# A two-layer trunk in float32: the down projection in pairs of column blocks with seven-product pairs, and the feed-forward stage in three parts

## The chip, the cores and the metric

The kernel runs on one core of one Trainium2 chip. A core has TensorE (matrix products), VectorE (elementwise work on two operands), ScalarE (casts, copies, activation functions), GpSimd, and SyncE, whose queue (SP) issues nearly all DMA transfers here. The metric is the time of one execution on the device in microseconds (us); lower is better.

## The reference

A trunk of two layers over 256 tokens of width 2048. Each layer is a normalised mixer with a residual add, and then a normalised SwiGLU feed-forward stage with a residual add. Layer 0 mixes with sliding-window attention and an mLSTM, layer 1 with a forgetting attention. Only the feed-forward stage is touched here:

```python
FFN_HIDDEN = -(-(8 * D_MODEL) // (3 * 256)) * 256      # 5632

def swiglu(xn, w_gate, w_up, w_down):
    return (jax.nn.silu(xn @ w_gate) * (xn @ w_up)) @ w_down
...
        h = h + mix.astype(h.dtype)
        h = h + swiglu(rms_norm(h, norm_ffn[layer]), w_gate[layer], w_up[layer], w_down[layer])
    return rms_norm(h, norm_final)
```

All weights and activations are float32: `w_gate` and `w_up` are 2048 x 5632 per layer, `w_down` is 5632 x 2048.

## The kernel before

**A product in float32.** Each float32 operand is split into a rounded part and the rest (`hi` and `lo` for weights, `xh`/`xl` or `mh`/`ml` for activations), and a product is made of three matmuls: high by high, high by low, low by high (`three`, line 344). The split of a weight chunk of two k blocks by 512 columns (`split_chunk`, line 138) is one ScalarE cast (L141) and one VectorE subtraction (L142), both 128x1024. The 256 tokens are two tiles of 128, `t` = 0 and 1. So one chunk of 2 x 128 rows by 512 columns of a weight takes 2 k blocks x 2 token tiles x 3 = 12 matmuls of 128x512.

**Tiles.** Raw weights are loaded by SP into the pool `wr` with four tiles of 512 KB (L87), the split halves lie in `wp` with six `hi` and six `lo` tiles. PSUM has eight banks, four in the pool `pa` and four in `pm`.

**Gate and up.** The hidden width of 5632 is 11 blocks of 512 columns (`g`). `gate_up` makes one block of both products at once, over 8 pairs of k blocks in the order given by `ORDER`. Five pairs are plain: a chunk of `w_gate` and a chunk of `w_up`, 24 matmuls. Three pairs are mixed (pairs 2, 3 and 6): the 2x2 block product (two token tiles by two k blocks, two k blocks by the two matrices) is made by the Strassen-Winograd scheme with seven block products of three matmuls, 21 matmuls. For that VectorE forms four differences of raw weights in the tile `t4` (L378 to L381), splits of these follow (`ht`, `lt`, L240 and L241), and the sums of activations `sh`, `sl` were made earlier in `sums_of`. The seven products go to the four `plain` accumulators and four banks `mixed`. After the last pair, L405 to L409 combine the four banks (L406 is the first of VectorE's) and L413 adds the plain ones; the result goes through SiLU, a product with the up half, and eight transposes, and is split into `mh`, `ml` (or `eh`, `el` for k blocks from 16 on). With `par` the roles of the pools `pa` and `pm` change from block to block: the plain accumulators of a block take the banks that the mixed products of the block before had.

**Down.** `HALVES = (0, 6, 11)` cuts the 11 hidden blocks into two parts. After the gate/up blocks of a part, its share of the down projection follows: for each of four column blocks of 512 `gemm` runs over the part's 24 or 20 k blocks with plain chunks into two accumulators, and `add_out` (L246) adds to `h` (in the last part of layer 1 `finish`, L824 and on, with the gain `gf` loaded by GpSimd's queue, L447).

**Order.** The source gives instructions in program order, and a scheduler of the framework orders them on each engine's queue when the program is built, by priority, dependencies and free tiles. At run time every queue runs strictly in that built order. So an instruction that waits holds all behind it on its engine, and a load that waits for a free tile on SP holds all later loads.

Of the kernel before, what the change touches and what calls it, by code (L numbers as in the profile page):

```python
# [10 lines left out]
ALU = mybir.AluOpType  # L11
# [23 lines left out]
MIXED = [p for w, p in ORDER if w]  # L35
HALVES = (0, 6, 11)
# [3 lines left out]
def trunk(  # L40
# [128 lines left out]
    def x_of(k):  # L169
        return xh[:, k, :], xl[:, k, :]  # L170
# [28 lines left out]
    def sums_of(extra, pair, src):  # L199
        sh, sl, pool = extra  # L200
        full = pool.tile([P, 2, NT, P], F32, tag="tmp", name="full")
        for i in range(2):
            g = src[1][i]
            nc.scalar.mul(full[:, i, :, :].rearrange("p t q -> p (t q)"), src[0][i], g)
# [5 lines left out]
        j = MIXED.index(pair)  # L210
        split_plain(sh[:, j, :, :], sl[:, j, :, :], s)

    def split_scaled(idx, n, extra=None):
        for half in range(2):
            pt = pm.tile([P, 2, NT, P], F32, tag="pm", name="pt")
            for i in range(2):
                k = 4 * n + 2 * half + i
                for t in range(NT):
                    nc.tensor.transpose(pt[:, i, t, :], h[:, t, k * P : (k + 1) * P], ident)
# [8 lines left out]
            if extra is not None and 2 * n + half in MIXED:  # L228
                k = 4 * n + 2 * half
                sums_of(  # L230
                    extra,
                    2 * n + half,
                    (
                        [pt[:, i, :, :].rearrange("p t q -> p (t q)") for i in range(2)],
                        [gT[:, idx * KT + k + i : idx * KT + k + i + 1] for i in range(2)],
                    ),
                )
# [114 lines left out]
    def gate_up(fp, sh, sl, layer, g, par):  # L352
        c0 = g * NB
        plain = [[bank(par, "acc") for _ in range(NT)] for _ in range(2)]
        mixed = None
        count = [s_[0] for s_ in ORDER]
        for pos, (w, pair) in enumerate(ORDER):
            k0 = 2 * pair
            if not w:
                for m, wt in enumerate((w_gate[layer], w_up[layer])):  # L360
                    hi, lo = load_chunk(wt, k0, c0, NB)
                    for i in range(CK):
                        ah, al = x_of(k0 + i)
                        for t in range(NT):
                            ts = slice(t * P, (t + 1) * P)
                            three(
                                plain[m][t], ah[:, ts], al[:, ts], hi[:, i, :], lo[:, i, :],
                                pos == 0 and i == 0, pos == len(ORDER) - 1 and i == CK - 1,
                            )
                continue  # L370
            first, last = 1 not in count[:pos], 1 not in count[pos + 1 :]
            if first:
                mixed = [bank(1 - par, "prod") for _ in range(4)]
# [4 lines left out]
            nc.vector.tensor_tensor(out=t4[:, 0, :], in0=ru[:, 0, :], in1=rg[:, 0, :], op=ALU.subtract)  # L378
            nc.vector.tensor_tensor(out=t4[:, 1, :], in0=ru[:, 1, :], in1=ru[:, 0, :], op=ALU.subtract)  # L379
            nc.vector.tensor_tensor(out=t4[:, 2, :], in0=ru[:, 1, :], in1=t4[:, 0, :], op=ALU.subtract)  # L380
            nc.vector.tensor_tensor(out=t4[:, 3, :], in0=rg[:, 1, :], in1=t4[:, 2, :], op=ALU.subtract)  # L381
            hu = wp.tile([P, CK, NB], F32R, tag="hi", name="hi")
            lu = wp.tile([P, CK, NB], F32R, tag="lo", name="lo")
            split_plain(hu[:, 1, :], lu[:, 1, :], ru[:, 1, :])
# [7 lines left out]
            j = MIXED.index(pair)  # L392
            xa, la = x_of(k0)
            xb, lb = x_of(k0 + 1)
            t0, t1 = slice(0, P), slice(P, 2 * P)
            three(mixed[0], xa[:, t0], la[:, t0], hg[:, 0, :], lg[:, 0, :], first, last)
            three(plain[0][0], xb[:, t0], lb[:, t0], hg[:, 1, :], lg[:, 1, :], False, False)
            three(plain[1][0], sh[:, j, 3, :], sl[:, j, 3, :], hu[:, 1, :], lu[:, 1, :], False, False)
            three(mixed[1], sh[:, j, 0, :], sl[:, j, 0, :], ht[0], lt[0], first, last)
            three(mixed[2], sh[:, j, 2, :], sl[:, j, 2, :], ht[1], lt[1], first, last)  # L400
            three(mixed[3], sh[:, j, 1, :], sl[:, j, 1, :], ht[2], lt[2], first, last)
# [3 lines left out]
        nc.scalar.copy(c[:, 0, :], mixed[0])  # L405
        nc.vector.tensor_tensor(out=u2, in0=mixed[3], in1=c[:, 0, :], op=ALU.add)  # L406
        nc.vector.tensor_tensor(out=c[:, 1, :], in0=mixed[2], in1=u2, op=ALU.add)
        nc.vector.tensor_tensor(out=c[:, 2, :], in0=mixed[1], in1=u2, op=ALU.add)
        nc.vector.tensor_tensor(out=c[:, 3, :], in0=mixed[1], in1=c[:, 1, :], op=ALU.add)  # L409
        for m in range(2):  # L410
            for t in range(NT):
                o = c[:, 2 * m + t, :]
                nc.vector.tensor_tensor(out=o, in0=plain[m][t], in1=o, op=ALU.add)  # L413
        return c

    def ffn(layer, fp, sh, sl, eh, el, key, idx_next=None, key_next=None, finish=None):
        def a_of(k):
            return m_of(k) if k < KT else (eh[:, k - KT, :], el[:, k - KT, :])

        r = rstd(key)  # L420
        for part in range(2):
            g0, g1 = HALVES[part : part + 2]
            nk = 4 * (g1 - g0)
            for g in range(g0, g1):
                par = (g - g0 + part) % 2
                c = gate_up(fp, sh, sl, layer, g, par)
# [6 lines left out]
                for half in range(2):  # L433
# [5 lines left out]
                    k = 4 * (g - g0) + 2 * half  # L439
                    if k < KT:  # L440
                        split_plain(mh[:, k : k + 2, :], ml[:, k : k + 2, :], pt)
                    else:
                        split_plain(eh[:, k - KT : k - KT + 2, :], el[:, k - KT : k - KT + 2, :], pt)
            gf = None
            if part == 1 and finish is not None:
                gf = fp.tile([P, D], F32, tag="t4", name="gf", bufs=1)
                nc.gpsimd.dma_start(gf, norm_final.partition_broadcast(P))  # L447
            wd = w_down[layer][4 * g0 * P : 4 * g1 * P, :]
            for n in range(4):
                acc = new_acc()  # L450
                end = part == 1 and idx_next is None and n == 3
                gemm(acc, a_of, wd, n * NB, NB, 0, nk, nk, skew=3 if end else 1)
                if part == 0:
# [7 lines left out]

    def close_layer(layer, w_out, idx, key, **rest):
        with tc.tile_pool(name=f"fp{layer}", bufs=2) as fp:
            deep = max(4 * (b - a) for a, b in zip(HALVES, HALVES[1:])) - KT
            eh = fp.tile([P, deep, S], F32R, name="eh", bufs=1)
            el = fp.tile([P, deep, S], F32R, name="el", bufs=1)
            sh = fp.tile([P, len(MIXED), 4, P], F32R, name="sh", bufs=1)
            sl = fp.tile([P, len(MIXED), 4, P], F32R, name="sl", bufs=1)
            out_proj(w_out, idx, key, (sh, sl, fp))
            ffn(layer, fp, sh, sl, eh, el, key, **rest)  # L470
# [419 lines left out]
```

## Time and profile before

| | |
|---|---|
| median of 3 runs | 2177.47 us (2176.23 to 2179.84) |
| the profiled execution, its own time | 2177.11 us |
| its span | 2175.4 us |
| mean granted TensorE clock | 0.998 |
| raw loads of `w_gate`, `w_up`, `w_down` | 176 each, 512 KB each |
| median time to landing of these | 3.6, 4.5, 3.7 us |
| bytes moved, mean rate | 408.34 MB, 188 GB/s |

The span runs from the first to the last instruction of the profiled execution; its own time is a little longer, for what lies around the span. An engine is busy while an instruction of it executes. TensorE's matmuls are pipelined, so that one starts before the one before it has ended, and a matmul's duration is longer than the step from one to the next.

The feed-forward stage of layer 0 lies at about 350 to 1062 us of the span, that of layer 1 from about 1455 us to the end. In each of them stretches of gate and up blocks (some 43 us a block) alternate with stretches of down projection.

### The profile page before, as it was taken

The page shows a single profiled execution, that of the slowest core. Times are in us where ns is not written, and L with a number is a line of the kernel's source. Part 1 is how long each engine was busy: PE and PEld are TensorE (multiplying, and loading weights), DVE is VectorE, ACT ScalarE, POOL GpSimd, SP SyncE. Part 2 cuts the span into 40 slices and gives each one's busy share as a digit, 9 for nine tenths or more (in the row PEclk, how much of TensorE's full clock was granted, in tenths as well). Part 3 has the DMA queues.
Part 4 walks back from the last instruction along what each step waited for, and adds up shares of the span by engine and source line. Part 5 has one row for each costly group of instructions (what it writes and reads, how often), then busy time and mean ns, then how long its engine had stood idle before and what let it go on. Part 6 is the DMA issues. An engine that isn't in the chain of part 4 may idle for free.

```text
span 2175.4 us, 26701 instructions
## 1 busy us (share of the span) xinstructions
PE 2152.4 (99%) x9986; PEld 1783.4 (82%) x9986; DVE 1526.5 (70%) x1874; ACT 1118.8 (51%) x1447; POOL 37.7 (2%) x61
## 2 busy tenths in 40 slices
PE   8999999999999999999999999999999999999998
PEld 7888888888888888888888888888877888888886
DVE  5565567899864688975555555678898745888953
ACT  6564455555543455554545444555555534555543
POOL 2110000000000000000010000000000000000000
PEclk9999999999999999999999999999999999999999
DMA  8444555656566665565575555556655666656663
GB/s 265 144 155 148 171 166 184 210 175 201 188 213 194 192 200 196 184 211 185 172 235 167 165 174 161 180 175 202 202 185 184 213 193 189 204 184 207 204 203 126
DMA packets 213539, 408.34 MB, mean 188 GB/s; under 512 B 12737, under 2 KB 21025, under 8 KB 213153
## 3 DMA queue, kind: packets, MB, share of 16 engines
q1 hardware_dynamic: 212736, 402.90, 58.1%
q0 software_dynamic: 624, 3.72, 0.5%
q8 instruction: 78, 1.28, 0.2%
q14 instruction: 53, 0.43, 0.1%
q10 hardware_dynamic: 48, 0.02, 0.0%
HBM read 404.48 MB, written 2.11 MB: 187 GB/s over the span
## 4 chain that ended last, share of the span: by engine, by line
PE 76%; DVE 13%; DMA 7%; issue 2%; ACT 1%; DVEq 0%; SPq 0%; ACTq 0%; POOLq 0%; POOL 0%
PE acc L166 17%; PE acc L165 17%; PE acc L164 17%; DMA raw<-in_w_up_dram 6%; PE acc L345 6%; PE acc L346 6%; PE acc L347 6%; DVE lo L142 4%; DVE lt L241 2%; PE prod L345 1%; PE prod L347 1%; PE prod L346 1%; DVE t L378 1%; DVE t L380 1%; DVE t L381 1%
## 5 line engine op out<-in xcount | busy, mean ns | idle before, releaser
L142 DVE TENSOR_TENSOR lo<-raw,hi 128x1024 fp32r<-128x1024 f32 (+3 forms) x710 | 850.9, 1202 | 490.1 <-ACT hi L141 487.5
L141 ACT CAST hi<-raw 128x1024 fp32r<-128x1024 f32 (+3 forms) x710 | 730.5, 1033 | 762.3 <-PE acc L166 484.0
L345 PE MATMUL acc<-hi,xh 128*128 128x512 f32 x946 | 368.0, 391 | 6.7 <-DVE u L406 6.6
L346 PE MATMUL acc<-lo,xh 128*128 128x512 f32 x946 | 369.2, 390 | 0.0
L347 PE MATMUL acc<-hi,xl 128*128 128x512 f32 x946 | 366.0, 390 | 0.0
L164 PE MATMUL acc<-hi,mh 128*128 128x512 f32 x768 | 300.3, 391 | 1.2 <-ACT mh L240 1.2
L165 PE MATMUL acc<-lo,mh 128*128 128x512 f32 x768 | 300.5, 391 | 0.0
L166 PE MATMUL acc<-hi,ml 128*128 128x512 f32 x768 | 298.8, 390 | 0.0
L164 PE MATMUL acc<-hi,xh 128*128 128x512 f32 (+3 forms) x736 | 276.6, 377 | 0.7 <-ACT hi L141 0.7
L166 PE MATMUL acc<-hi,xl 128*128 128x512 f32 (+3 forms) x736 | 276.8, 377 | 0.0
L165 PE MATMUL acc<-lo,xh 128*128 128x512 f32 (+3 forms) x736 | 276.2, 375 | 0.0
L345 PEld LDWEIGHTS acc<-hi,xh 128*128 128x128 f32 x946 | 177.6, 188 | 47.5 <-DVE u L406 11.0
L347 PEld LDWEIGHTS acc<-hi,xl 128*128 128x128 f32 x946 | 177.6, 188 | 36.6
L346 PEld LDWEIGHTS acc<-lo,xh 128*128 128x128 f32 x946 | 177.6, 188 | 36.3 <-DVE lo L142 0.2
L240 ACT CAST ht<-t 128x1024 fp32r<-128x1024 f32 x132 | 136.7, 1049 | 76.8 <-DVE t L379 46.2
L164 PEld LDWEIGHTS acc<-hi,mh 128*128 128x128 f32 x768 | 144.2, 188 | 31.2 <-ACT mh L240 1.5
L165 PEld LDWEIGHTS acc<-lo,mh 128*128 128x128 f32 x768 | 144.2, 188 | 29.5
L166 PEld LDWEIGHTS acc<-hi,ml 128*128 128x128 f32 x768 | 144.2, 188 | 29.5
L241 DVE TENSOR_TENSOR lt<-t,ht 128x1024 fp32r<-128x1024 f32 x132 | 158.6, 1217 | 4.4 <-ACT ht L240 4.2
L164 PEld LDWEIGHTS acc<-hi,xh 128*128 128x128 f32 x736 | 138.9, 189 | 24.8 <-ACT hi L141 1.1
L166 PEld LDWEIGHTS acc<-hi,xl 128*128 128x128 f32 x736 | 139.0, 189 | 24.5 <-issue 0.8
L165 PEld LDWEIGHTS acc<-lo,xh 128*128 128x128 f32 x736 | 139.1, 189 | 24.0 <-issue 0.7
(273 smaller groups left out, 2217.4 us busy)
## 6 DMA issues: line engine op xcount, KB each, us to landing
raw<-in_w_gate_dram SPq DMA_DIRECT2D x176, 512.0 KB, 3.6
raw<-in_w_up_dram SPq DMA_DIRECT2D x176, 512.0 KB, 4.5
raw<-in_w_down_dram SPq DMA_DIRECT2D x176, 512.0 KB, 3.7
raw<-in_w_in_odd_dram SPq DMA_DIRECT2D x88, 512.0 KB, 3.8
raw<-in_w_in_even_dram SPq DMA_DIRECT2D x64, 512.0 KB, 4.1
raw<-in_w_out_even_dram SPq DMA_DIRECT2D x32, 512.0 KB, 3.7
raw<-in_w_out_odd_dram SPq DMA_DIRECT2D x32, 512.0 KB, 3.7
raw<-in_w_in_odd_dram SPq DMA_DIRECT2D x8, 272.0 KB, 2.8
```

What stands on the lines that cost most here:

```text
L141: nc.scalar.copy(hi[:, :, 0:n], raw[:, :, 0:n])
L142: nc.vector.tensor_tensor(out=lo[:, :, 0:n], in0=raw[:, :, 0:n], in1=hi[:, :, 0:n].bitcast(F32), op=ALU.subtract)
L164: nc.tensor.matmul(o, ah[:, ts], hi, start=(k == 0), stop=False)
L165: nc.tensor.matmul(o, ah[:, ts], lo, start=False, stop=False)
L166: nc.tensor.matmul(o, al[:, ts], hi, start=False, stop=(k == k_all - 1))
L240: nc.scalar.copy(dst_h, src)
L241: nc.vector.tensor_tensor(out=dst_l, in0=src, in1=dst_h.bitcast(F32), op=ALU.subtract)
L345: nc.tensor.matmul(o, ah, hi, start=start, stop=False)
L346: nc.tensor.matmul(o, ah, lo, start=False, stop=False)
L347: nc.tensor.matmul(o, al, hi, start=False, stop=stop)
L378: nc.vector.tensor_tensor(out=t4[:, 0, :], in0=ru[:, 0, :], in1=rg[:, 0, :], op=ALU.subtract)
L380: nc.vector.tensor_tensor(out=t4[:, 2, :], in0=ru[:, 1, :], in1=t4[:, 0, :], op=ALU.subtract)
```

## The change

`gate_up` becomes a general `pair_group`, which takes two weight matrices (or two column blocks of one), the activations and an order of pairs, and returns the plain accumulators and the combined products. Gate and up use it as before. The down projection uses it too, for two neighbouring column blocks at a time: of the 6 pairs of k blocks in a part of three hidden blocks one is mixed, of the 8 pairs in a part of four two are. Only the last two column blocks of layer 1 stay with `gemm`. The feed-forward stage has three parts, `PARTS = (0, 3, 7, 11)`, so that a part's activations have at most 16 k blocks and `eh`, `el` go. The activation sums for the down projection's mixed pairs, `sd`, are made by `sums_of` right after the split of a hidden block. The two raw tiles of a mixed pair come from the pool `fp` (two tiles) and no longer from `wr`. The plain accumulators of the last pair are finished one token tile after the other. At the end of a column group VectorE adds the combined products to `h` (four operations) and then the plain accumulators (`add_out`), where before there was one add for each. The load of `gf` now stands behind the first column group of layer 1's last part.

```diff
-MIXED = [p for w, p in ORDER if w]
-HALVES = (0, 6, 11)
+DOWN = {
+    6: ((0, 0), (0, 1), (1, 2), (0, 3), (0, 4), (0, 5)),
+    8: ((0, 0), (0, 1), (1, 2), (0, 3), (0, 4), (1, 5), (0, 6), (0, 7)),
+}
+PARTS = (0, 3, 7, 11)
...
-    def load_raw(w, k0, c0, n):
-        raw = wr.tile([P, CK, NB], F32, tag="raw", name="raw")
+    def load_raw(w, k0, c0, n, pool=wr):
+        raw = pool.tile([P, CK, NB], F32, tag="raw", name="raw")
...
-    def gate_up(fp, sh, sl, layer, g, par):
+    def pair_group(fp, par, lhs, sums, mats, order):
...
+                last = pos == len(order) - 1
+                walk = [(i, t) for i in range(CK) for t in range(NT)]
+                if last:
+                    walk.sort(key=lambda it: it[1])
+                for m, (w, c0) in enumerate(mats):
+                    hi, lo = load_chunk(w, k0, c0, NB)
+                    for i, t in walk:
...
-            rg = load_raw(w_gate[layer], k0, c0, NB)
-            ru = load_raw(w_up[layer], k0, c0, NB)
-            hg, lg = split_chunk(rg, NB)
+            ra, rb = (load_raw(w, k0, c0, NB, fp) for w, c0 in mats)
+            hg, lg = split_chunk(ra, NB)
...
-        for part in range(2):
-            g0, g1 = HALVES[part : part + 2]
+        for g0, g1 in zip(PARTS, PARTS[1:]):
+            end = g1 == PARTS[-1]
             nk = 4 * (g1 - g0)
+            order = DOWN[nk // 2]
             for g in range(g0, g1):
-                par = (g - g0 + part) % 2
-                c = gate_up(fp, sh, sl, layer, g, par)
+                par = (g1 - 1 - g) % 2
+                plain, c = pair_group(
+                    fp, par, x_of, sums_x, [(w_gate[layer], g * NB), (w_up[layer], g * NB)], ORDER
+                )
...
+                    split_plain(mh[:, k : k + 2, :], ml[:, k : k + 2, :], pt)
+                    if pair in mixed_of(order):
+                        j = mixed_of(order).index(pair)
+                        sums_of(
+                            fp, sd[0][:, j, :, :], sd[1][:, j, :, :], lambda full, pt=pt: nc.scalar.copy(full, pt)
+                        )
...
-            for n in range(4):
-                acc = new_acc()
-                end = part == 1 and idx_next is None and n == 3
-                gemm(acc, a_of, wd, n * NB, NB, 0, nk, nk, skew=3 if end else 1)
...
+            for n0 in (0, 2):
+                if end and idx_next is None and n0 == 2:
+                    for n in (2, 3):
+                        acc = new_acc()
+                        gemm(acc, m_of, wd, n * NB, NB, 0, nk, nk, skew=3 if n == 3 else 1)
+                        close(acc, n)
+                    continue
+                plain, c = pair_group(
+                    fp, 1 - n0 // 2, m_of, sums_d, [(wd, n0 * NB), (wd, (n0 + 1) * NB)], order
+                )
+                if end and idx_next is None:
+                    gf = fp.tile([P, D], F32, tag="t4", name="gf", bufs=1)
+                    nc.gpsimd.dma_start(gf, norm_final.partition_broadcast(P))
+                for m in range(2):
+                    for t in range(NT):
+                        o = h[:, t, (n0 + m) * NB : (n0 + m + 1) * NB]
+                        nc.vector.tensor_tensor(out=o, in0=c[:, 2 * m + t, :], in1=o, op=ALU.add)
+                for m in range(2):
+                    close(plain[m], n0 + m)
```

Here `close` calls `add_out`, or `finish` at the end of layer 1, and at the end of layer 0 also `split_scaled` and `square_sum` for the next layer's input.

More of the change, by code (lines that the diff above doesn't have):

```diff
@@ L227, in split_scaled, with copies @@
                 )
[L228 to L237, printed above, removed]
+            pair = 2 * n + half
+            if extra is not None and pair in mixed_of(ORDER):
+                sh, sl, pool = extra
+                j = mixed_of(ORDER).index(pair)
+                def copies(full):
+                    for i in range(2):
+                        g = gT[:, idx * KT + 2 * pair + i : idx * KT + 2 * pair + i + 1]
+                        nc.scalar.mul(full[:, i, :], pt[:, i, :, :].rearrange("p t q -> p (t q)"), g)
+                sums_of(pool, sh[:, j, :, :], sl[:, j, :, :], copies)
     def split_plain(dst_h, dst_l, src):
@@ L358, in gate_up @@
             k0 = 2 * pair
[L359 to L369, printed above, removed]
+            if not kind:
+                last = pos == len(order) - 1
[5 more added lines that the diff above has]
+                    for i, t in walk:
+                        ah, al = lhs(k0 + i)
+                        ts = slice(t * P, (t + 1) * P)
+                        three(
+                            plain[m][t], ah[:, ts], al[:, ts], hi[:, i, :], lo[:, i, :],
+                            pos == 0 and i == 0, last and i == CK - 1,
+                        )
@@ L370, in gate_up @@
                 continue
-            first, last = 1 not in count[:pos], 1 not in count[pos + 1 :]
+            first, last = 1 not in kinds[:pos], 1 not in kinds[pos + 1 :]
             if first:
-                mixed = [bank(1 - par, "prod") for _ in range(4)]
-            rg = load_raw(w_gate[layer], k0, c0, NB)
-            ru = load_raw(w_up[layer], k0, c0, NB)
-            hg, lg = split_chunk(rg, NB)
+                prods = [bank(1 - par, "prod") for _ in range(4)]
+            ra, rb = (load_raw(w, k0, c0, NB, fp) for w, c0 in mats)
@@ L438, in ffn, with sums_d, close @@
                             nc.tensor.transpose(pt[:, i, t * P : (t + 1) * P], c[:, t, cs : cs + P], ident)
[L439 to L448, printed above, removed]
-            for n in range(4):
-                acc = new_acc()
-                end = part == 1 and idx_next is None and n == 3
-                gemm(acc, a_of, wd, n * NB, NB, 0, nk, nk, skew=3 if end else 1)
-                if part == 0:
+                    pair = 2 * (g - g0) + half
+                    k = 2 * pair
+                    split_plain(mh[:, k : k + 2, :], ml[:, k : k + 2, :], pt)
[4 more added lines that the diff above has]
+                        )
+            def sums_d(pair, order=order):
+                j = mixed_of(order).index(pair)
+                return sd[0][:, j, :, :], sd[1][:, j, :, :]
+            def close(acc, n):
+                if not end:
                     add_out(acc, n)
```

90 lines of the change are left out of this document (45 added, 45 removed).

## The prediction

> **What bounds the kernel now.** The page's head and totals come first, then the waits of TensorE (PE), then two stretches, then instructions in order of time. In the waits the columns are: who waited for whom, us in total, times, longest us. In the stretches: length, then busy time of PE, weight load, VectorE (DVE), ScalarE (ACT) and GpSimd with instruction counts, TensorE's granted clock, DMA share, GB/s. The third fence has start, us, engine, line, operation.
>
> ```profile
> span 2175.4 us, 26701 instructions
> PE 2152.4 (99%) x9986; PEld 1783.4 (82%) x9986; DVE 1526.5 (70%) x1874; ACT 1118.8 (51%) x1447; POOL 37.7 (2%) x61
> ...
> PE acc L345 <- DVE u L406: 6.6, 9, 1.6
> PE pg L128 <- DMA gn<-in_norm_mix_dram: 3.9, 1, 3.9
> PE pt L219 <- DMA h<-in_x_dram: 1.3, 2, 1.1
> PE acc L164 <- ACT mh L240: 1.2, 1, 1.2
> ```
>
> ```profile
> 567.00:610.00 43.00, 42.90 (x193) 35.24 (x192) 38.35 (x47) 23.34 (x27) 0.00 (x0) 1.00 0.61 204
> 610.00:740.00 130.00, 130.00 (x579) 107.67 (x578) 70.46 (x68) 53.94 (x53) 0.00 (x0) 1.00 0.61 192
> ```
>
> ```profile
> 473.87 1.22 DVE L241 TENSOR_TENSOR lt<-t,ht 128x1024 fp32r<-128x1024 f32 x1
> 475.01 1.22 DVE L142 TENSOR_TENSOR lo<-raw,hi 128x1024 fp32r<-128x1024 f32 x1
> ...
> 476.88 0.68 DVE L379 TENSOR_TENSOR t<-raw 128x512 f32<-128x512 f32 x1
> 477.48 0.68 DVE L380 TENSOR_TENSOR t<-raw,t 128x512 f32<-128x512 f32 x1
> 478.08 1.21 DVE L142 TENSOR_TENSOR lo<-raw,hi 128x1024 fp32r<-128x1024 f32 x1
> 479.22 0.68 DVE L381 TENSOR_TENSOR t<-raw,t 128x512 f32<-128x512 f32 x1
> 479.82 1.21 DVE L241 TENSOR_TENSOR lt<-t,ht 128x1024 fp32r<-128x1024 f32 x1
> 480.96 0.68 DVE L406 TENSOR_TENSOR u<-prod,c 128x512 f32<-128x512 f32 x1
> ...
> 476.83 0.39 PE L346 MATMUL prod<-lt,sh 128*128 128x512 f32 x1
> 477.06 0.39 PE L347 MATMUL prod<-ht,sl 128*128 128x512 f32 x1
> ...
> 480.91 0.39 PE L347 MATMUL acc<-hi,xl 128*128 128x512 f32 x1
> 481.69 0.50 PE L345 MATMUL acc<-hi,xh 128*128 128x512 f32 x1 [0.39 <-DVE u L406]
> ```
>
> TensorE is idle 2175.4 - 2152.4 = 23.0 us: the four waits shown (13.0) and one of 0.7, and some 9 after the last matmul. So its own work sets the time, at a clock of 1.00. A matmul is entered with 0.39 us, but they overlap: from 477.06 to 480.91 17 steps take 3.85 us, **0.2265 us for a 128x512 matmul**. VectorE starts its next operation 0.60 us after a 512-wide one (476.88, 477.48) and 1.14 us after a 1024-wide one (478.08, 479.22). Gate/up groups (first stretch) hold VectorE at 0.89 of the time, the down projection (second stretch) at 0.54.
>
> The 6.6 us in L345 have one cause. A group's first matmul takes a PSUM bank that the group before frees in L406. In the excerpt VectorE does 5.8 us of other work between the last `lt` and L406; TensorE has 19 matmuls (4.3 us) between its first use of that `lt` and the next group. With L406 the run is 6.5 us, so 2.2 us must come from VectorE's lead (end of `lt`, 475.09, to its first matmul, 476.83: 1.74), and about 0.4 is missing.
>
> **The change, step by step.**
>
> Matmuls removed. A mixed pair takes 7 products of 3 matmuls, 21 where two plain chunks take 24. One of six pairs is mixed in a part of three hidden blocks, two of eight in a part of four, over two column groups: layer 0 has 2 + 4 + 4 such pairs, layer 1 2 + 4 + 2 (its last two column blocks stay plain). 18 x 3 = 54 matmuls; the built programs have 8730 and 8676 of this shape. 54 x 0.2265 = **-12.2 us**, all on the path.
>
> VectorE and ScalarE added. 204 operations 512 wide: 18 x 5 for differences and one split, 11 column groups x 8 for combining products and adding to `h`, 16 in `add_out` for the third part, 10 splits of sums. With 18 more 1024 wide (20.5 us) and 40 of 128x128 (0.28 us each, L206, 11): 204 x 0.60 + 20.5 + 11 = 154 us of VectorE. ScalarE gets 18 casts of 1.05 and 49 copies of some 0.6: 48 us, in an engine at 0.51. What hides them is TensorE: an eight-pair column group is 186 matmuls, 42.1 us, against 12 x 1.14 + 2 x (2 x 1.14 + 1.14 + 5 x 0.60) + 12 x 0.60 = 33.7 us, 0.80; a six-pair group 31.9 against 25.0, 0.78; a gate/up group stays at 0.89. Taken at nothing as work; as lateness it is priced next.
>
> The PSUM wait. The same run can be counted in the built order of the new kernel for each of its 33 groups. At 12 gate/up groups VectorE has four `lo`, four differences and L406 (7.6 us) and TensorE 29 matmuls (6.6): a lead of 1.1 us is needed. At 6 it is 0.5, at 4 (the last gate/up group of a four-block part, before the down projection) 2.1, at 2 (from a six-pair column group to the next gate/up group, 20.5 against 17.5 us) 3.1; elsewhere none. In the old order ten transitions need 2.2 and four 1.5; the ten cost 6.6 us, which makes the mean lead 1.5. With that lead the old waits go, **-6.6**; the four need 0.6 more each, **+2.4**. For the two the bounds are 0 and 1.6 each; I take 0.5, **+1.0**, since over a run of 20 us the lead can be rebuilt, which the short runs do not allow.
>
> [...]
>
> Loads. SP issues as many as before (748 of 512 KB). The raws of mixed pairs move from the four shared tiles to two of their own, so plain loads keep four; a mixed load now waits on SP for the mixed pair before it, and behind it wait all later loads, then ScalarE's casts and the differences. In the built order the next plain loads stand ahead of such mixed loads. TensorE has not waited on a load of weights (waits above); taken at nothing, bounds in the rivals.
>
> Moved past the ends. (a) The 1 MB load of the final gain (8.3 us to landing, 0.6 to issue) now follows the last mixed pair; between that pair's last `lt` and the first use VectorE has eight `lo` and nine 512-wide operations, 14.5 us, which covers 8.9. Without that cover the later `lo` would stand behind the gain and TensorE could lose up to 8.9. (b) At the end of layer 0 two column blocks close together: after the last matmul come an add (0.68), a square (0.63), a scaling (0.47) and a subtraction (0.48), 2.3 us, before the first new input; TensorE has 16 transposes (0.1 each) and 48 matmuls 272 wide (their starts stand 0.13 apart in the timeline just after layer 0 now), some 7.8 us. Nothing; uncovered, 2.3. (c) One more boundary of parts per layer: the down projection starts with products two or three blocks old; its PSUM wait is counted above.
>
> Sum: -12.2 - 6.6 + 2.4 + 1.0 = **-15.4 us**. Span 2175.4 - 15.4 = 2160.0; the profiled run took 2177.11, 1.7 over its span, and the median is 0.36 above it: **2162.0 us**.
>
> **Rivals.**
>
> 1. VectorE's lead shrinks to 1.0 us, since the down stretch at 0.54, in which it ran ahead, is now at 0.8. Waits: 12 x 0.1 + 4 x 1.1 + 2 x 2.1 = 9.8; 2177.5 - 18.8 + 9.8 = 2168.5. For it: in the old kernel the first two transitions after a calm stretch never wait. Against: four full groups in a row at 0.89 still left 1.5.
>
> 2. The other side: the lead goes altogether. All transitions wait in full: 12 x 1.1 + 6 x 0.5 + 4 x 2.1 + 2 x 3.1 = 30.8; -18.8 + 30.8 = +12, 2189.5. It decides from a lead of 0.5 us, where the waits come to 18.8. For it: no group of a feed-forward stage is below 0.78 any more. Against: the smallest lead in the old trace is 2.2 - 1.6 = 0.6, and 0.80 of 42 us leaves 8 us per column group to catch up.
>
> 3. The two raw tiles of mixed pairs become the wait. In a gate/up group mixed pairs come every 45 matmuls, 10.2 us. The tiles are held for four differences, a `lo` and a half `lo` (4.1 us), and the next load takes 4.5 to land plus two issues of 0.37: 9.4 us, hidden; with two plain `lo` in between 11.7, or 1.5 us at 44 places, +66, 2225. It turns slower above 10.6 us. Against: six `hi` and `lo` tiles and the plain pairs between let TensorE go on.
>
> 4. The matmuls removed were not what paces TensorE, and the time stays at 2177. For it stands the weight load's 82% beside 99%; against it the even 0.2265 us at both.
> [...]
>
> **How the numbers follow.** Forecast 0.66, rival 1 0.14, rival 2 0.10, rival 3 0.03, rival 4 0.03, in between 0.04. The measurement tells 0.2% (4.4 us) from no change: faster is below 2173.1. Forecast, rival 1 and half the rest give 0.82 faster; rivals 2 and 3 less a part that ends near break-even 0.11 slower; 0.07 the same. The range: no PSUM wait gives 2158.7, and runs scatter 1.2 below the median, 2157; a lead of 0.9 gives waits of 11.6, 2170.3, and runs scatter 2.4 above, 2173. That leaves out rivals 2 to 4 and little else, under 2 in 10.
>
> **What would show it.** 54 fewer matmuls at the same 0.2265 us; VectorE's busy time up by 150 to 170 us; TensorE's wait for the operation that is now L413 at some 3.4 us, at the groups before a down projection; no wait for `hi`, `lo` or a load. Wrong if TensorE waits more than 10 us in the feed-forward stages, for whichever cause, or if the matmul's step grows.

## The result, and the profile after

The changed kernel takes 2155.02 us, the median of 4 runs (2154.62 to 2155.24), against 2178.65 us for the kernel before on the same chip (4 runs, 2176.23 to 2179.94): a ratio of 0.9893 [0.9875, 0.991]. A second set on another occasion gave 2154.89 us and 0.9887 [0.9869, 0.9905]. The forecast was faster, 2162.0 us in 2157 to 2173; the direction held, and the time lies 2 us below the range. The profiled execution took 2154.99 us with a span of 2153.3 us, 22.1 us less than the span before. Where spans are compared below, they are those of profiled executions.

The page's head and totals of the changed kernel, then TensorE's waits (who waited for whom, us in total, times, longest us):

```profile
span 2153.3 us, 27002 instructions
...
PE 2137.1 (99%) x9932; PEld 1774.6 (82%) x9932; DVE 1668.7 (77%) x2136; ACT 1164.1 (54%) x1514; POOL 37.7 (2%) x61
```

```profile
PE pg L137 <- DMA gn<-in_norm_mix_dram: 4.0, 1, 4.0
PE acc L173 <- ACT mh L246: 1.2, 1, 1.2
PE pt L224 <- DMA h<-in_x_dram: 1.1, 1, 1.1
PE acc L173 <- ACT hi L150: 0.7, 1, 0.7
PE pp L318 <- DVE s L310: 0.2, 1, 0.2
```

The page counts 54 matmuls fewer and 262 VectorE instructions more, as forecast. The line for the PSUM banks, 6.6 us in nine waits before, is not there any more, and nothing has taken its place: no line of the feed-forward stage is left. The forecast had expected 3.4 us of waits to remain, in L413.

Two stretches of the changed kernel (columns as in the prediction): a gate and up group of a four-block part with its end, then two column groups of the down projection.

```profile
665.00:711.00 46.00, 46.00 (x208) 38.16 (x207) 42.38 (x55) 26.34 (x30) 0.00 (x0) 1.00 0.59 192
711.00:787.00 76.00, 76.00 (x340) 62.91 (x340) 64.73 (x78) 39.27 (x43) 0.00 (x0) 1.00 0.60 196
```

VectorE is busy for 0.92 of the first and 64.73 / 76 = 0.85 of the second, where the down stretch before had 0.54. TensorE is busy throughout at a clock of 1.00. So VectorE did lose its calm stretch, as rival 2 said; yet its lead did not go. It grew. The excerpt is the transition at the end of that gate and up group, in order of time; the next group's first matmul is the one at 711.26:

```profile
699.45 2.59 DVE L247 TENSOR_TENSOR lt<-t,ht 128x1024 fp32r<-128x1024 f32 x2 [0.58 <-ACT ht L246]
...
706.28 0.39 PE L352 MATMUL prod<-lt,sx 128*128 128x512 f32 x1
...
709.07 0.68 DVE L413 TENSOR_TENSOR u<-prod,c 128x512 f32<-128x512 f32 x1
...
711.04 0.39 PE L353 MATMUL acc<-hi,xl 128*128 128x512 f32 x1
...
711.26 0.39 PE L351 MATMUL acc<-hi,mh 128*128 128x512 f32 x1
```

The last `lt` is ready at 699.45 + 2.59 = 702.04, and its first matmul runs at 706.28: a lead of 4.24 us where 2.1 is needed by the forecast's count. L413 frees its bank at 709.75, 1.5 us before the bank is used, and the step from 711.04 to 711.26 is an even 0.22 us. Read in the same way, the ten old transitions that waited had leads of 1.07 to 3.04 us, 2.1 in the mean; all new ones that need a lead have 4.2 us or more.

Why the lead grew is not seen in TensorE's waits at all. It is seen in those of ScalarE and VectorE for raw weight tiles. Before:

```profile
ACT hi L141 <- DMA raw<-in_w_gate_dram: 59.5, 55, 2.1
ACT hi L141 <- DMA raw<-in_w_up_dram: 35.9, 47, 1.9
ACT hi L240 <- DMA raw<-in_w_up_dram: 28.4, 14, 2.9
DVE t L378 <- DMA raw<-in_w_up_dram: 21.3, 24, 2.4
ACT hi L141 <- DMA raw<-in_w_down_dram: 19.2, 18, 1.9
```

After:

```profile
DVE t L386 <- DMA raw<-in_w_up_dram: 45.4, 30, 4.2
DVE t L386 <- DMA raw<-in_w_down_dram: 7.5, 8, 1.6
...
ACT hi L150 <- DMA raw<-in_w_down_dram: 5.0, 2, 4.2
...
ACT hi L150 <- DMA raw<-in_w_up_dram: 1.8, 1, 1.8
```

They fall from 164.3 to 59.7 us. ScalarE's casts of gate and up weights, 59.5 + 35.9 + 28.4 = 123.8 us of it, have 1.8 left. TensorE waits for none of these loads itself, but late loads made the split halves late: ScalarE's cast at 2008.79 us in the old kernel waited 0.93 us for a load of `w_up`, and VectorE then 0.58 us for that cast. Over the whole span VectorE's waits for `hi` are 487.5 us in 419 times before (L142) and 285.9 us in 266 times after (L151). Loads in turn waited for raw tiles: before, SP stood from 774.86 to 782.70 us, 7.8 us, in front of a load until a `lo` was done, and issued no other in that time. In the old kernel some of the waits for loads also lie in the very stretch that the forecast counted as work without a stop, from a group's last `lt` to L406. The old transition with the longest of the ten leads, 3.04 us, shows it:

```profile
2009.88 1.23 DVE L142 TENSOR_TENSOR lo<-raw,hi 128x1024 fp32r<-128x1024 f32 x1 [0.58 <-ACT hi L141]
2011.96 0.69 DVE L378 TENSOR_TENSOR t<-raw 128x512 f32<-128x512 f32 x1 [0.86 <-DMA raw<-in_w_up_dram]
...
2016.65 0.68 DVE L406 TENSOR_TENSOR u<-prod,c 128x512 f32<-128x512 f32 x1
```

VectorE stands idle for 0.58 + 0.86 = 1.44 us here, and TensorE then waits 0.58 us for L406. In eight of the ten transitions VectorE was idle in this stretch, for 0.46 to 1.44 us, and in all eight part of it was the load of `w_up` at L378.

The 22.1 us can be taken apart in the timeline. Over all neighbouring 128x512 matmuls, the starts stood 27.0 us further apart in all than 0.2267 us a step before, and 17.0 us after: 10.0 us less. The 54 matmuls are 12.2. Together they are 22.2 us. Of the 10.0, 9.4 are the ten old PSUM waits (nine that the waits list, and a tenth too short for it).

### The profile page after: what moved, and what is told of

Same layout as the page of the kernel before. It is cut to its first block, busy times and chain, and to the rows that moved or that the text cites. A ratio compares the mean times of both kernels' runs of the same rounds, so it can differ in the third digit from the quotient of the medians.

```text
span 2153.3 us, 27002 instructions
## 1 busy us (share of the span) xinstructions
PE 2137.1 (99%) x9932; PEld 1774.6 (82%) x9932; DVE 1668.7 (77%) x2136; ACT 1164.1 (54%) x1514; POOL 37.7 (2%) x61
## 4 chain that ended last, share of the span: by engine, by line
PE 98%; ACT 1%; issue 0%; DMA 0%; DVE 0%; DVEq 0%; POOLq 0%; POOL 0%; ACTq 0%
PE acc L353 17%; PE acc L352 17%; PE acc L351 17%; PE acc L173 10%; PE acc L175 10%; PE acc L174 10%; PE prod L353 4%; PE prod L352 4%; PE prod L351 4%; PE pf L450 1%; PE pt L224 1%; PE p L275 1%; PE ptm L258 1%; PE po L326 1%; PE pp L318 0%
## 5 line engine op out<-in xcount | busy, mean ns | idle before, releaser
L150 ACT CAST hi<-raw 128x1024 fp32r<-128x1024 f32 (+1 forms) x692 | 707.5, 1033 | 648.5 <-PE acc L353 314.3
L151 DVE TENSOR_TENSOR lo<-raw,hi 128x1024 fp32r<-128x1024 f32 (+1 forms) x692 | 825.7, 1201 | 288.1 <-ACT hi L150 285.9
L247 DVE TENSOR_TENSOR lt<-t,ht 128x1024 fp32r<-128x1024 f32 x168 | 200.1, 1219 | 28.8 <-ACT ht L246 27.8
L246 ACT CAST ht<-t 128x1024 fp32r<-128x1024 f32 x168 | 174.6, 1053 | 81.1 <-PE prod L353 44.3
L352 PE MATMUL acc<-lo,mh 128*128 128x512 f32 x514 | 200.4, 390 | 0.0
L353 PE MATMUL acc<-hi,ml 128*128 128x512 f32 x514 | 199.4, 389 | 0.0
L351 PE MATMUL acc<-hi,mh 128*128 128x512 f32 x514 | 198.9, 389 | 0.0
L173 PE MATMUL acc<-hi,mh 128*128 128x512 f32 x320 | 125.8, 393 | 1.2 <-ACT mh L246 1.2
L174 PE MATMUL acc<-lo,mh 128*128 128x512 f32 x320 | 125.7, 393 | 0.0
L175 PE MATMUL acc<-hi,ml 128*128 128x512 f32 x320 | 124.0, 390 | 0.0
```

Source lines behind the costliest of these rows:

```text
L150: nc.scalar.copy(hi[:, :, 0:n], raw[:, :, 0:n])
L151: nc.vector.tensor_tensor(out=lo[:, :, 0:n], in0=raw[:, :, 0:n], in1=hi[:, :, 0:n].bitcast(F32), op=ALU.subtract)
L173: nc.tensor.matmul(o, ah[:, ts], hi, start=(k == 0), stop=False)
L174: nc.tensor.matmul(o, ah[:, ts], lo, start=False, stop=False)
L175: nc.tensor.matmul(o, al[:, ts], hi, start=False, stop=(k == k_all - 1))
L246: nc.scalar.copy(dst_h, src)
```

## The experiments

Theory A, formed from this: the two raw tiles of their own let loads start earlier, splits come earlier, VectorE's lead grows, and the PSUM waits go; the mixed pairs of the down projection then add their 12.2 us undisturbed. Its rival B: the new order did it (three parts, column groups, other transitions), and the raw tiles were of no account. Further rivals stand in the expectations.

| run | median us | ratio to before | span us | load waits in the feed-forward stages, us |
|---|---|---|---|---|
| changed kernel | 2155.02 | 0.9893 [0.9875, 0.991] | 2153.3 | 60 |
| the same again | 2154.89 | 0.9887 [0.9869, 0.9905] | 2153.5 | 53 |
| mixed raws back in the shared tiles | 2164.48 | 0.9927 [0.9911, 0.9944] | 2167.6 | 242 |
| no mixed pair in down | 2167.86 | 0.9949 [0.9934, 0.9963] | 2167.1 | 49 |
| three parts and raw tiles, first bank order | 2208.89 | 1.0136 [1.0121, 1.0152] | 2206.2 | 38 |
| three parts, first bank order | 2226.75 | 1.0216 [1.0201, 1.0231] | 2225.7 | 136 |
| three parts and raw tiles | 2167.38 | 0.9944 [0.9928, 0.9959] | 2165.7 | 41 |
| three parts alone | 2175.06 | 0.9984 [0.9974, 0.9993] | 2172.5 | 139 |
| second mixed pair in six | 2152.81 | 0.9878 [0.9862, 0.9894] | 2150.9 | 54 |
| differences made three times | 2228.57 | 1.0217 [1.02, 1.0235] | 2231.6 | 234 |
| three shared raw tiles | 2156.22 | 0.9895 [0.988, 0.991] | 2155.3 | 192 |
| three of eight pairs mixed | 2195.39 | 1.0069 [1.0052, 1.0086] | 2187.4 | 231 |
| the added work elsewhere | 2169.76 | 0.9961 [0.9947, 0.9975] | 2168.4 | 45 |

**The raw tiles undone.** The changed kernel with one argument taken away:

```diff
-            ra, rb = (load_raw(w, k0, c0, NB, fp) for w, c0 in mats)
+            ra, rb = (load_raw(w, k0, c0, NB) for w, c0 in mats)
```

> The changed kernel with one part undone: the raws of mixed pairs lie in the four shared tiles again. 8676 matmuls of 128x512 as in the changed kernel. Theory A (the two raw tiles let loads come earlier, and this is what gives VectorE its lead of 4 to 6 us and ends the PSUM waits): ScalarE's and VectorE's waits on loads of the feed-forward weights go back from some 60 us towards the 164 us of the kernel before, the lead at the third and later gate/up groups falls from 4 to 6 us to 1 to 3 us. The built order needs only 1.1 to 1.5 us there, so TensorE waits little: span 2153 to 2158. Theory B (the shorter parts and the column groups between them rebuild the lead): leads stay at 4 to 6 us, waits on loads stay near 60 us, span 2153.

2164.48 us (2160.99 to 2169.28): 9.5 us of the gain are gone, and the same work on every engine remains. That is more than either theory expected: theory A had a span of up to 2158 and load waits that go back towards 164 us, and they are 242. TensorE's waits in the feed-forward stage, and the two largest waits for loads:

```profile
PE acc L352 <- DVE lo L151: 3.5, 3, 1.8
PE acc L351 <- DVE u L413: 2.3, 5, 0.5
```

```profile
ACT hi L150 <- DMA raw<-in_w_down_dram: 67.8, 51, 3.6
ACT hi L150 <- DMA raw<-in_w_gate_dram: 61.6, 48, 3.1
```

The wait for L413 is back at five transitions; at four of them, the last gate and up group before a down projection, the lead is 0.93 to 1.32 us. That is the place that the forecast had named, with 2.3 us where it had 3.4. At three of these four TensorE waits just before for a `lo` as well, 3.5 us in all, of which the forecast had nothing. So it is partly luck that its 2162.0 us came near to the time of this kernel, the one without the two tiles. The eight waits, 5.8 us as listed, cost 8.0 us in distances of starts, and behind two pairs of them the clock fell, which cost 3.1 us more (last section). In all the steps give 29.9 - 17.0 = 12.9 of the 14.3 us by which the span is longer. The profiled execution is the slowest of the four.

**Mixed pairs taken out of the down projection.** Three parts, column groups and raw tiles stay; all pairs of `DOWN` are plain, and 8730 matmuls of 128x512 are issued as before.

```diff
-    6: ((0, 0), (0, 1), (1, 2), (0, 3), (0, 4), (0, 5)),
-    8: ((0, 0), (0, 1), (1, 2), (0, 3), (0, 4), (1, 5), (0, 6), (0, 7)),
+    6: ((0, 0), (0, 1), (0, 2), (0, 3), (0, 4), (0, 5)),
+    8: ((0, 0), (0, 1), (0, 2), (0, 3), (0, 4), (0, 5), (0, 6), (0, 7)),
...
```

> The changed kernel with every pair of the down projection plain (8730 matmuls), column groups, parts and raw tiles kept; no activation sums, no combining in the down projection. If 54 matmuls are worth 12.2 us and their VectorE work nothing: span 2153.3 + 12.2 = 2165.5. If the mixed pairs cost hidden time that the lead hides only in part, less: under 2164.

2167.86 us. The span is 13.8 us longer than the changed kernel's (12.9 by the medians), 12.2 of which are the matmuls. TensorE waits for nothing of the feed-forward stage here either, so what made the PSUM waits go is not the mixed pairs.

**Parts and raw tiles without column groups.** The kernel before, with three parts and the mixed pairs' raws in `fp`; and then the parts alone, with four shared raw tiles.

```diff
-HALVES = (0, 6, 11)
+HALVES = (0, 3, 7, 11)
...
-            rg = load_raw(w_gate[layer], k0, c0, NB)
-            ru = load_raw(w_up[layer], k0, c0, NB)
+            rg = load_raw(w_gate[layer], k0, c0, NB, fp)
+            ru = load_raw(w_up[layer], k0, c0, NB, fp)
...
-        for part in range(2):
+        for part in range(3):
...
-                par = (g - g0 + part) % 2
+                par = (g1 - 1 - g) % 2
...
```

> The kernel before (down projection plain, 8730 matmuls) with three parts and the two raw tiles of their own. No mixed pair in the down projection. Both theories: no PSUM wait, the 9.3 us of it gone, span 2175.4 - 9.3 = 2166, some 0.5 less for the steps that no longer stand out of order. If the waits go only through the new column groups: 2170 or more.

> The kernel before with three parts alone: down projection plain, four shared raw tiles, 8730 matmuls. The built order still has four transitions that need 2.2 us of lead (in the kernel before ten). Theory A: leads of 1 to 3 us, these four wait 0.9 us each, 3.7 us in all, so 2175.4 - 5.6 = 2170. Theory B (short parts alone keep the lead): no wait, 2166.

Both missed: 2208.89 and 2226.75 us, slower than before. The first of TensorE's waits names the cause:

```profile
PE pf L438 <- DVE c L430: 31.6, 6, 7.3
```

Six waits of up to 7.3 us, one at the end of each part: the transposes of a part's last block stand next in TensorE's queue and wait for the block's SiLU and product, instead of matmuls of the down projection coming first. `par` is the changed kernel's here, made for column groups that choose their banks themselves; the plain down projection always takes banks of `pa`, and with this `par` a part's last block holds them. So these two runs say nothing on A and B. The other bank order, in one line:

```diff
-                par = (g1 - 1 - g) % 2
+                par = (g1 - g) % 2
```

> The changed kernel unaltered, so that the three below are compared with it on one chip. Span 2153 to 2156, no wait of TensorE in the feed-forward stages, waits on loads of feed-forward weights some 60 us.

> The kernel before with three parts and two raw tiles for mixed pairs (8730 matmuls), and with the PSUM pools of the gate/up blocks alternating so that the last block of each part has its plain accumulators in pm, as in the kernel before, since the plain down projection accumulates in pa. Theory A (the raw tiles end the PSUM waits): leads 5 to 6 us, no PSUM wait, 9.3 us less than the kernel before: span 2166 (up to 2168 on a chip as slow as that of the first experiments). If the bank order was not what made the runs e2_parts_and_raws and e3_parts_only slow: again over 2200.

> As the one before but with four shared raw tiles: three parts alone. The built order has four transitions that need 2.2 us of lead (the kernel before ten). Theory A: leads of 1 to 3 us there, the four wait 0.9 us each: 3.7 us of waits, span 2170 (to 2172). Theory B (short parts alone keep the lead): no PSUM wait, the same span as e2b_parts_raws.

The line L438 is gone from both, and the spans fall by 40.5 and 53.2 us. Parts alone: 2175.06 us, 0.16% below before; the span of 2172.5 us lies just above what theory A expected. Parts and raw tiles: 2167.38 us, with the span that theory A expected. The waits for loads of the two, parts alone first:

```profile
ACT hi L141 <- DMA raw<-in_w_down_dram: 34.4, 29, 2.6
ACT hi L141 <- DMA raw<-in_w_gate_dram: 34.1, 33, 2.7
ACT hi L141 <- DMA raw<-in_w_up_dram: 30.7, 37, 2.0
DVE t L378 <- DMA raw<-in_w_up_dram: 28.3, 28, 2.5
```

```profile
DVE t L378 <- DMA raw<-in_w_up_dram: 38.5, 40, 3.1
...
ACT hi L141 <- DMA raw<-in_w_down_dram: 2.4, 2, 2.1
```

With the two tiles ScalarE's plain casts nearly stop waiting, the leads of the third and fourth block of each part go from 1.3 to 3.5 us up to 5.15, and the waits on L406 (1.4 us in three, with the parts alone) go. With the parts alone TensorE also waits 3.9 us at the start of the two stages, twice for `xl` and twice for `lt`, and in neither of the kernels beside it, so the shares of the two steps are not sharp. By the medians of one set the change adds up so: 2179.17 us before; 2175.06 with the parts (-4.1, B's share); 2167.38 with the two raw tiles (-7.7, A's share); 2154.89 with column groups and mixed pairs (-12.5, against 12.2 for 54 matmuls). In spans the three steps are -2.9, -6.8 and -12.4.

**One pair more in the small groups.** A second mixed pair of six, 12 matmuls fewer.

```diff
-    6: ((0, 0), (0, 1), (1, 2), (0, 3), (0, 4), (0, 5)),
+    6: ((0, 0), (0, 1), (1, 2), (0, 4), (1, 3), (0, 5)),
```

> The changed kernel with a second mixed pair in the down projection of the three-block part (two of six), so 4 more mixed pairs and 12 fewer matmuls: 8664. VectorE in those column groups goes from 0.78 to 0.93 of TensorE's time. If VectorE's lead of 4 to 6 us holds: 2.7 us less than the changed kernel on the same chip. Rival 2 of the prediction (the lead goes when no calm stretch is left): PSUM waits come back at the transitions out of these groups (need 1.7 us), and the span is the same or longer.

2152.81 us (2152.19 to 2153.78), below the changed kernel's 2154.89 in the same set. The span is 2.4 us shorter, against 12 x 0.2265 = 2.7. Leads stay at 4.2 us or more. This is the fastest of all runs.

**How far it carries.** Three runs push VectorE and the raw tiles. The first makes the four differences of each mixed pair of the down projection three times over, 144 operations (86 us) more on VectorE.

```diff
+            for _ in range(3 if lhs is m_of else 1):
-            nc.vector.tensor_tensor(out=t4[:, 0, :], in0=rb[:, 0, :], in1=ra[:, 0, :], op=ALU.subtract)
+                nc.vector.tensor_tensor(out=t4[:, 0, :], in0=rb[:, 0, :], in1=ra[:, 0, :], op=ALU.subtract)
...
```

The second takes one shared raw tile away (five in all), and the third has three mixed pairs of eight and two of six; as there is no room for its activation sums otherwise, it too has three shared raw tiles.

```diff
-    wr = ctx.enter_context(tc.tile_pool(name="wr", bufs=4))
+    wr = ctx.enter_context(tc.tile_pool(name="wr", bufs=3))
```

```diff
-    8: ((0, 0), (0, 1), (1, 2), (0, 3), (0, 4), (1, 5), (0, 6), (0, 7)),
+    8: ((0, 0), (0, 1), (1, 2), (0, 4), (1, 3), (0, 6), (1, 5), (0, 7)),
```

> The changed kernel with the four differences of each mixed pair of the down projection formed three times over (same values): 18 x 8 = 144 more VectorE operations of 0.60 us, 86 us. An eight-pair column group then holds VectorE for 43.3 us against 42.2 of TensorE, a six-pair group 29.8 against 32.0. Theory A (VectorE's lead comes from loads that are early enough, and is rebuilt in the gate/up groups at 0.89): the lead in the column groups shrinks, PSUM and split waits come to 0 to 8 us, span 2153 to 2161. Rival 2 of the prediction (the lead lives on calm stretches and goes with them): 20 us of waits and more, span over 2173.

> The changed kernel with three shared raw tiles for plain chunks in place of four (mixed pairs keep their two): five raw tiles in all, between the four and the six of the other kernels. If it is the separate tiles for mixed pairs that matter: leads of 4 to 6 us, no waits, span 2153. If it is the number of raw tiles: waits on loads between the 60 us of the changed kernel and the 240 of e1_shared_raws, leads of 1 to 4 us where the built order needs up to 4.0 us, TensorE waits of 3 to 15 us, span 2156 to 2168.

> The changed kernel with two of six and three of eight pairs of the down projection mixed, 29 such pairs, 8643 matmuls, 33 fewer; the activation sums of the third pair need 4 KB a partition, which the fourth shared raw tile gives up. TensorE alone would give 7.5 us less: 2146. VectorE is at 0.85 to 0.98 of TensorE's time between group ends. If three shared tiles do (see e9_three_shared) and the lead holds: 2146. If either fails: 2150 to 2165.

With five tiles alone, 2156.22 us: one short wait for `lo` (0.8 us), and leads of 2.25 us and more, though load waits are 192 us. That lies between the two outcomes that were expected. So a sum of load waits alone does not tell the time; what counts is whether a lead is left where one is needed. Three of eight pairs mixed, 33 matmuls fewer (7.5 us), on the same five tiles: 2195.39 us, a miss for both expected values. Tripled differences: 2228.57 us, far over what theory A expected and where rival 2 had it. TensorE's first waits and the first two for loads in that run:

```profile
PE prod L351 <- ACT ht L246: 11.4, 14, 3.9
PE acc L351 <- ACT hi L150: 8.8, 7, 3.1
PE prod L352 <- DVE lt L247: 8.0, 14, 1.1
PE acc L351 <- DVE u L414: 5.6, 5, 2.1
```

```profile
ACT hi L150 <- DMA raw<-in_w_down_dram: 78.9, 41, 5.8
ACT hi L150 <- DMA raw<-in_w_gate_dram: 64.4, 26, 4.7
```

Here the lead is gone, as in rival 2: at ten transitions, from 756 us on, the last `lt` is ready 0.06 us before its matmul starts. In the run with three of eight it is 0.06 to 0.81 us at nine. But the run with tripled differences changed two things at once. VectorE had more to do, and the raw tiles were held 8 operations longer, so that loads came late. The last run has the same 144 operations at the same mixed pairs, after the last reading of the raw tiles, into a tile that nobody reads:

```diff
             split_plain(hu[:, 1, :], lu[:, 1, :], rb[:, 1, :])
+            if lhs is m_of:
+                u3 = fp.tile([P, NB], F32, tag="tmp", name="u3")
+                for _ in range(8):
+                    nc.vector.tensor_tensor(out=u3, in0=h[:, 0, 0:NB], in1=h[:, 1, 0:NB], op=ALU.add)
```

> The changed kernel with 144 further VectorE adds of 512 elements, 8 in each of the 18 mixed pairs of the down projection, on tiles that no load and no matmul waits for, placed after the mixed pair's last reading of its two raw tiles. The amount is that of the run with tripled differences (2228.6 us; 144 operations, 86 us), but there the raw tiles were held until the last of them. Theory T (that run lost its time because raw tiles came free late, and with them the loads, 234 us of load waits against 60): the time stays at 2155 to 2175, with less than 120 us of load waits. Rival V (what counts is VectorE's time wherever it lies: an eight-pair column group goes from 33.7 to 43.3 us of it against 42.1 of TensorE): VectorE falls behind in the same way, 2205 to 2235, with waits of TensorE for lt and u as in that run.

2169.76 us (2169.46 to 2170.79), inside what the raw tiles' theory expected and 59 us below the run with the same work on held tiles. Its totals, TensorE's waits that are new, and the waits for loads:

```profile
PE 2143.1 (99%) x9932; PEld 1777.5 (82%) x9932; DVE 1750.8 (81%) x2280; ACT 1163.0 (54%) x1514; POOL 35.8 (2%) x61
```

```profile
PE pt L224 <- DVE h L252: 4.2, 1, 4.2
...
PE acc L351 <- DVE u L417: 2.6, 2, 1.3
PE acc L351 <- ACT hi L150: 2.3, 2, 1.1
```

```profile
DVE t L386 <- DMA raw<-in_w_up_dram: 21.7, 22, 3.3
ACT hi L150 <- DMA raw<-in_w_down_dram: 14.0, 14, 2.0
```

VectorE is as busy (1750.8 us, 1753.5 with tripled differences), yet leads stay at 2.08 us or more and load waits at 45 us. Of the 15.1 us more than the changed kernel's span, 9.1 are the three waits shown; the largest, at the end of layer 0, is the place (b) of the forecast, which was hidden in the changed kernel and comes out once VectorE is late there. So of the 78 us that tripled differences cost in span, 15 would be VectorE's time, and the rest came with the place of the work. That it came through raw tiles held longer is not shown, since the place changed a further thing: the differences themselves are ready later, and ScalarE's cast to `ht` waits for them and holds the casts behind it. With tripled differences these waits are the following and one more of 26.4 us:

```profile
ACT ht L246 <- DVE t L390: 54.6, 31, 4.2
ACT ht L246 <- DVE t L388: 28.1, 14, 6.8
```

That is 109 us, against 29 us with the added work elsewhere and 15 us in the changed kernel. No run holds the raw tiles longer without delaying the differences. Besides, each kernel is scheduled anew, so that the two orders also differ in other places.

Three more things stay open. Whether three of eight pairs would pay with six raw tiles was not tried, for want of room, and neither were six shared tiles, or mixed pairs in the last two column blocks of layer 1.

## Why the prediction was partly right

**Right: the matmuls.** 54 fewer at an unchanged step. In spans, the parts and raw tiles alone against the changed kernel give 12.4 us, the changed kernel without its mixed pairs 13.8, the 12 matmuls of the second pair in six 2.4, against 12.2, 12.2 and 2.7. That also settles rival 4, for which the time would have stayed. The weight load's share is 82% in both kernels, and the time followed the number of matmuls, so that the 18% left were no headroom here.

**Right: the work added is hidden.** 262 VectorE operations more, as counted; its busy time rose by 142 us, a little less than the 150 to 170 forecast, and ScalarE's by 45 (48 forecast). None of it shows on TensorE. The ends (a) to (c), taken at nothing, show no wait either; that (b) hung on VectorE's slack was seen in the last run, 4.2 us where the forecast had 2.3 as uncovered.

**Wrong: the loads, "taken at nothing".** The prediction asked only whether TensorE waited for a load. It did not; but ScalarE and VectorE did, for 164 us, and that made the lead short and the stretch from the last `lt` to L406 long. With two more raw tiles these waits are 60 us in the changed kernel. The two tiles are worth 7.7 us beside the parts alone and 9.5 us in the changed kernel, both at the median (6.8 and 14.3 in the profiled spans). Rival 3 looked at the same tiles for a loss only, a new wait, and not for what the four shared tiles gain when mixed pairs leave them.

**Wrong in consequence: the PSUM term.** "With that lead the old waits go, -6.6; the four need 0.6 more each, +2.4", and +1.0 for the other two: the mean lead of 1.5 us was worked out from idle time, as if VectorE ran without a stop up to L406, and it was carried over from a kernel with other loads. Read directly, the old leads were 2.1 us in the mean, and VectorE's own stops, up to 1.44 us, made up the difference. With leads of 4.2 us and more in the changed kernel the 3.4 did not come. With the tiles shared again, waits on L413 came back at the transitions forecast, 2.3 us of them. So the rule named the right places, and its input was that of another kernel.

**Mis-sized: what the old wait cost.** The 6.6 us are the idle time listed. In the prediction's own excerpt the matmul at 481.69 is entered as 0.39 us late, but starts 0.78 us after the one before, 0.55 more than an even step, and the step after it is 0.11 too long. Over the nine listed waits that is 8.07 + 1.00 = 9.1 us, and a tenth too short to be listed makes it 9.4. The term was -9.4 and not -6.6 + 3.4 = -3.2. With it the sum is -12.2 - 9.4 = -21.6, against -22.1 measured; the rest is smaller steps elsewhere, not followed up. This also is why the range's lower end, worked out with no PSUM wait left, was not low enough.

**The rivals.** 1 did not come: leads grew. 2 came in neither size nor sign, but the lead did go, with the waits that it named, when the kernel was pushed. 3 did not come: TensorE waits for no load in the feed-forward stages.

## What to carry to other kernels

An engine that never waits for loads can still be held by them through others: here TensorE waited for none in the feed-forward stages, ScalarE and VectorE for 164 us, and two raw tiles more were worth 7.7 and 9.5 us. Before a buffer's price is set at nothing, look at the waits of the engines that feed the bound engine, above all inside the stretches that it waits for, and ask how much lead they would have without them. Their sum alone does not tell: 192 us of them cost next to nothing where a lead was left (2156.22 us beside 2155.02). A lead read in one kernel must not be carried to one in which the loads start at other times: 2.1 us in the mean before, 4.2 us and more in the changed kernel. And cost a wait of TensorE by the distance of starts, not by the idle time listed; in these runs the first was 1.4 times the second.

## What the runs showed of the hardware, unexpected

Matmuls released after a wait started later than the idle time says: 9.1 us of lost start distance for 6.6 us of listed idle time at nine waits before, the following step included, which was longer by 0.11 us each time. With the tiles shared again it was 8.0 us for 5.8 us at eight waits.

After the four waits of 6.7 to 7.3 us on L438 TensorE ran at a lower clock for a while. Stretches around the first of them in the run with three parts, raw tiles and the first bank order (485.00 is where the wait of 6.7 us ends; the clock is the number before the last two):

```profile
475.00:478.00 3.00, 3.00 (x15) 2.41 (x13) 3.00 (x4) 1.06 (x1) 0.00 (x0) 1.00 0.74 239
478.00:485.00 7.00, 0.30 (x3) 0.00 (x1) 7.00 (x11) 2.49 (x3) 0.00 (x0) 0.71 0.49 147
485.00:487.00 2.00, 2.00 (x6) 1.71 (x7) 0.61 (x1) 0.00 (x0) 0.00 (x0) 0.50 0.53 205
487.00:489.00 2.00, 2.00 (x8) 1.59 (x8) 0.00 (x0) 0.00 (x0) 0.00 (x0) 0.82 0.00 0
```

At a clock of 0.50 the matmuls started 0.43 us apart in place of 0.2265, until 2.7 to 4.8 us after the end of each of the four waits; after the two of 1.6 us the steps stayed even. The slow steps add some 6.7 us to the 31.6 us of idle time, so that the waits come to 38.3 of the 40.5 us by which the span is longer than with the other order. Behind the wait of 6.7 us the clock was 0.50, and 1.00 again from about 487.7 us on, 2.7 us after its end (an estimate from the 0.82 of the last row: 0.7 us at 0.50 and 1.3 us at 1.00).

Shorter waits that stood close together were followed by slow steps too. With the raw tiles shared again, waits of 1.17 and 0.47 us were followed by eight slow steps at a clock of 0.50, and so were waits of 1.84 and 0.47 us. With tripled differences, where the clock was 0.95 over 950 to 1060 us, slow steps came after a wait of 2.83 us, and at 1039 us after several of which none was longer than 1.1 us. They did not come each time: with the added work elsewhere, waits of 1.13 and 1.32 us were followed by eight slow steps in layer 0, and the same pair in layer 1 by none.

The place of VectorE's work mattered more here than its amount: 144 operations, 86 us, cost 15 us of span where they held no raw tile and no difference of weights, and 78 us where two raw tiles were held, and the differences late, until they were done. Which of the two did it is open.
